# A two-layer hybrid trunk on one core: the second norm stepped into the output product, the second MLP product in another order, the query and key gains in the rotation tables

## The chip, the cores and the metric

The kernel runs as one program on one core of a Trainium2 chip. The metric is the device time of one execution in microseconds. Before the change three runs gave 3245.07, 3245.28 and 3249.05 us, a median of 3245.28 us.

## The reference

The model has two layers over 1024 latent and 256 context tokens of width 1024. Cut to what matters here:

```python
u = modulate(rms_norm(h, norm1_g), shift, scale)
pa, pb, pc, pd = split(u @ w_in)                 # SSD, GQA, RG-LRU, differential attention
q = rms_norm(q.reshape(b, L, H, d), q_g)         # per head; the same for k; for pb and pd
q, k = axial_rope(q, row, col), axial_rope(k, row, col)      # latent tokens only
...
mix = concat([ya, yb, yc, yd]) @ w_out
h = h + mod[2] * mix
v = modulate(rms_norm(h, norm2_g), mod[3], mod[4])
h = h + mod[5] * (square(relu(v @ w_mlp1)) @ w_mlp2)         # D_FF = 4096
```

Context tokens go through the same weights in layer 0 and, for what the latent tokens read of them, in layer 1. All values are float32.

## The kernel before

All work is first recorded as a list of operations and then put in order by a planner, the class `Sched`. The planner gives every operation a cost and a due time: the due time of a TensorE operation is the sum of the TensorE costs recorded before it, and other operations get theirs back from the operations that use their results. It then walks through simulated time, gives each free engine the ready operation that is due first, and emits the instructions in the order so found. So the order of recording isn't the order of execution, but it sets who is due first. All instructions carry line 606, since one helper emits them; they are told apart by tile names.

Tiles come from classes with a fixed number of slots: "S" has 30 wide tiles (1288 columns), "w" six for split weights, "raw" three for weights as loaded, "h" four of 512 columns. A class has quotas by stream of use (line 658 and the following), and a tile may be placed only if enough slots stay free for tiles of other streams that were recorded earlier and aren't placed yet. PSUM banks are given out by stream in the same way.

Every float32 product is made of three products in the fast float32 format: an operand is split into an upper part (`hi`, a copy, on ScalarE or VectorE) and the remainder (`lo`, a subtraction on VectorE), and hi*hi, hi*lo and lo*hi are added up in a PSUM bank. The residual stream h is held as eight tiles hT[k] of 128 features by up to 1280 tokens; tokens come in three groups, 0 and 1 of 512 latent tokens and 2 of 256 context tokens.

The parts that the change touches:

- `attn_proj` (line 1347) computes the projections dtq, kv, dq and dk in tiles of 128 tokens, and `qk_post` (line 1297) does the norm and the rotation of a tile: square on ScalarE, the product of the bank with the gain into b (line 1306), the sum of squares, the power -1/2 on GpSimd, and for latent tokens (t < 8) the products of b with the cosine and the sine table, their sum, the transposes and the split.
- `out_proj` (line 1531) is run twice; the second run ("w2367") holds all eight weight blocks split in the tiles wo and then goes through the groups 0, 1, 2 (0, 1 in layer 1), eight output tiles f in each.
- `norm_halves` (line 1596) follows it. `norm_stats` squares hT and sums over the features with small products, takes the power on GpSimd; `norm_rows` broadcasts the result into a bank. Then the operands of the seven products V0 to V6 of a Strassen-like scheme (2 by 2 by 2 blocks: two feature halves, two token halves) are made: X from group 0, Y from group 1 (tiles vx and vy), V0 and V1 are X, V4 a part of Y, and V2, V3, V5, V6 are differences. In layer 0 the context's operands stand in the last 256 columns of V0, V1, V2 and V4, and their temporaries lx come from class "h".
- `mlp_up` (line 1652) goes through 16 pairs p of column blocks of the first MLP weight. A pair loads two raw tiles, a11 and a12 in one, a21 and a22 in the other, makes the combinations in mt and in place, and does the seven products in the order V0 to V6 of 12 matmuls each, in layer 0 two context products of 24 matmuls of 256 columns as well. Tiles ma, mt, mc and mx of class "h" hold partial sums. Results go to DRAM (hp, hc).
- `mlp_down` (line 1767) does the second product in four quarters q of eight weight blocks, with the seven products named A11, A12, S3, A22, S2, S1, S4 and, for the context, A21. Accumulators are 14 wide tiles ka; operands kb (quota 7) are loaded through hs and split, context operands kc (4) are loaded as they are, weights stand in raw and kr (5). In the last quarter the sums of the accumulators and the additions to h follow, and h is reloaded (`reload_h`, line 1861) from the copy he.
- `mlp` (line 1882) saves h to he, calls `norm_halves`, records the constants of layer 1 in layer 0 (`consts_a`, `consts_b`: rows vrow, of class "h", transposed) and sets the modulation of layer 1 as filling: `raw_tile` takes 0.9 steps of it at every weight load.

Of the kernel before, what the change touches and what calls it, by code (L numbers as in the profile page):

```python
# [647 lines left out]
class Trunk:  # L648
# [4 lines left out]
    def __init__(self, tc, nc, A, out, pools, dbg=None):  # L653
# [4 lines left out]
        s.cls("S", sb, 30, SW, dict(u=16, ssd=8, lru=11, sw=2, qk=4, qv=2, ssdr=1, gk=4, dk=4, gv=2, dv=1, gq=2, dq=1, mo=2, gP=4, dP=8, gT=5, dT=5, mix=16, hT=8, wo=8, v=28, vx=4, vy=4, md=2, ka=14, kb=7, kr=5, kc=4, x=7, wm=10, st=5))  # L658
# [4 lines left out]
        s.psum(ps, dict(mm=(0, 1, 2, 3), m4=(0, 1, 2, 3, 4, 5), ln=(4, 5, 3), att=(3, 0), tr=(6, 7), pv=(6,), ax=(6,),  # L663
# [306 lines left out]
    def norm_stats(self, gi):  # L970
        s = self.s
# [3 lines left out]
        for k in range(0, 8, 2):  # L975
            calls = []
            for j in (k, k + 1):
                sq = s.tile("h", 512, F32, "lq", "sq")
                s.act(sq[:, 0:gn], self.hT[j][:, g0:g0 + gn], AF.Square)
                q = 32 * (j % 4)  # L980
                calls.append(dict(out=st[q:q + 32, 0:gn], lhsT=self.ones32, rhs=sq[:, 0:gn], start=(k < 4),
                                  stop=(k >= 4)))
            s.mms(calls, par=2)
        sts = s.tile("h", 512, F32, "lq", "sts")
# [7 lines left out]
        return m  # L992
# [304 lines left out]
    def qk_post(self, l, bank, off, H, d, gain, t, dst, rq=None):  # L1297
# [8 lines left out]
        s.tt(hd(b), hd(src), gain.un(1).bc([128, H, d]), ALU.mult)  # L1306
# [7 lines left out]
        if t < 8:  # L1314
            j = d // 4
            o = 144 * t + (0 if d == 64 else 96)
            cs = self.rope[:, o:o + d // 2]
            sn = self.rope[:, o + d // 2:o + d + d // 2]
            b4, c4, s4 = (v.r("p (h f k) -> p h f k", h=H, f=2) for v in (b, c, st[:, 0:n]))
            s.tt(c4, b4, cs.un(1).un(1).bc([128, H, 2, 2 * j]), ALU.mult)  # L1320
            s.tt(s4, b4[:, :, ::-1], sn.r("p (f k) -> p f k", f=2).un(1).bc([128, H, 2, 2 * j]), ALU.mult)
            s.tt(b, c, st[:, 0:n], ALU.add)
        y = b
# [23 lines left out]
    def attn_proj(self, l, u, name, tiles):  # L1347
# [6 lines left out]
        v = None  # L1354
        for t in tiles:
            yield (t - tiles[0]) / len(tiles)
            bank = self.gemm_tm(ww, u, t, n, 8 if name == "dtq" and t >= 8 and l == 1 else n)
            if name == "dtq":
                s.copy("ACT", dtraw[:, 8 * t:8 * t + 8], bank[:, 0:8])
                if t < 8 or l == 0:  # L1360
                    self.qk_post(l, bank, 8, 4, 64, L["gqa_q_norm_g"], t, self.qd["gq"], self.rq[:, 12 * t:12 * t + 4])
            elif name == "kv":
                self.qk_post(l, bank, 0, 2, 64, L["gqa_k_norm_g"], t, self.qd["gk"])
                v = self.put_v(v, t, bank[:, 128:256], self.qd["gv"])
            elif name == "dq":
                self.qk_post(l, bank, 0, 8, 32, L["diff_q_norm_g"], t, self.qd["dq"], self.rq[:, 12 * t + 4:12 * t + 12])
            elif name == "dk":
                self.qk_post(l, bank, 0, 8, 32, L["diff_k_norm_g"], t, self.qd["dk"])
# [162 lines left out]
    def out_proj(self, l, gis, ks):  # L1531
# [28 lines left out]
        for f in range(8):  # L1560
# [6 lines left out]
            if late:  # L1567
# [4 lines left out]
                held.append((hi, lo))  # L1572
            else:
# [22 lines left out]
    def norm_halves(self, l, gis):  # L1596
# [21 lines left out]
        bb = self.norm_rows(self.norm_stats(0), 0)  # L1618
        X, Y = [], []
        for k in range(4):  # L1620
            x = s.tile("S", SW, F32, "vx", "vx")
            X.append((x[:, 0:512], x[:, 512:1024]))
# [3 lines left out]
        bb = self.norm_rows(self.norm_stats(1), 1)  # L1626
        bc = self.norm_rows(self.norm_stats(2), 2) if 2 in gis else None
        for k in range(4):
            y = s.tile("S", SW, F32, "vy", "vy")
            Y.append((y[:, 0:512], y[:, 512:1024]))  # L1630
            for j in range(2):
                scaled(Y[k][j], k + 4 * j, 512, 512, 0, bb)
            s.tt(X[k][0], Y[k][0], X[k][0], ALU.subtract)
            put(2, k, X[k][0], None)
            put(4, k, Y[k][1], sh(0, k + 4))
            if bc is not None:
                for j in range(2):
                    z = s.tile("h", 512, F32, "ln", "lx")
                    scaled(z[:, 0:256], k + 4 * j, NL, 256, 1, bc)
                    hi, lo = V[j][k][:, 1024:1280], V[4 - 2 * j][k][:, 1024:1280]  # L1640
                    s.act(hi, z[:, 0:256], AF.Identity, bias=sh(1, k + 4 * j))
                    s.stt(lo, z[:, 0:256], sh(1, k + 4 * j), hi.f, ALU.add, ALU.subtract)
        for k in range(4):
            s.tt(X[k][0], Y[k][1], X[k][0], ALU.subtract)
            put(3, k, X[k][0], sh(0, k + 4))
            s.tt(Y[k][0], Y[k][1], Y[k][0], ALU.subtract)
            put(5, k, Y[k][0], dsh[:, k:k + 1])
            s.tt(X[k][1], X[k][1], X[k][0], ALU.subtract)
            put(6, k, X[k][1], None)
        return V  # L1650

    def mlp_up(self, l, V, gis):


        s, A = self.s, self.A
        w = A["w_mlp1"][l]
        self.hp, self.hc = [], []

        def product(bank, ws, o, first):
            wh, wl = ws  # L1660
            more = {} if first else {"skip_group_check": True}
            for k in range(4):
                c = slice(128 * k, 128 * k + 128)
                xh, xl = V[o][k][:, 0:512], V[o][k][:, 512:1024]
                s.mms([dict(out=bank.v, lhsT=wh[:, c], rhs=xh, start=(first and k == 0), stop=False, **more),
                       dict(out=bank.v, lhsT=wh[:, c], rhs=xl, start=False, stop=False, **more),
                       dict(out=bank.v, lhsT=wl[:, c], rhs=xh, start=False, stop=(first and k == 3), **more)])
# [8 lines left out]
        def context(e, w0, w1, ctx):  # L1676
            pb = bank()
# [15 lines left out]
        for p in range(16):  # L1693
            A2 = []
            for e in range(2):
                raw = self.raw_tile("wr")
                c0 = 128 * (2 * p + e)
                s.dma(raw[:, 0:1024].r("p (k c) -> p k c", k=8), w[:, c0:c0 + 128].rearrange("(k p) c -> p k c", p=128))
# [356 lines left out]
```

## Time and profile before

| | us |
|---|---|
| runs (median of three) | 3245.28 |
| the profiled execution | 3245.98 |
| its span | 3244.2 |
| TensorE busy in the span | 3096.8 |
| VectorE busy | 2434.1 |
| ScalarE busy | 1460.2 |

The span runs from the first to the last instruction of the profiled execution; 1.8 us of its time lie outside. Busy time counts an instruction from its start to its end, with overlaps counted once. [...] Names as in `wa<-wr` are tiles, written and read; a wait is put down to the instruction that released it.

### The profile page before, as it was taken

Reading aid. Unit: us, or ns where it says so; the run is one execution under the profiler, and the core shown is the slowest. Engines: PE = TensorE matmul, PEld = TensorE weight load, DVE = VectorE, ACT = ScalarE, POOL = GpSimd, SP = SyncE. Lnnn points to the kernel's source line nnn. Section 1 sums busy time; section 2 is a strip of 40 time slices with the busy share of each in tenths; the row PEclk is TensorE's granted clock in tenths of the full one; section 3 lists DMA queues with packets and bytes.
Section 4 is the critical chain, followed back from the end, with each engine's and each line's share of the span. In section 5 each row is a group of like instructions: output and inputs, shape, how many; then the busy total and the mean of one; then the engine's idle time right before and its main releaser. Section 6 shows DMA issues by size and latency. Waiting matters only on the chain. (4 is left out here: it accounts for less than half of the span.)

```text
span 3244.2 us, 47231 instructions
## 1 busy us (share of the span) xinstructions
PE 3096.8 (95%) x17688; PEld 2483.1 (77%) x17688; DVE 2434.1 (75%) x4451; ACT 1460.2 (45%) x2658; POOL 148.9 (5%) x168
## 2 busy tenths in 40 slices
PE   8999999899979999999999999999999899999998
PEld 6877886677757777888887688786677577877886
DVE  4797789895476566666779689689895587777888
ACT  5555438774143223343323474347783333345333
POOL 0020040000000000000000010030000000000000
PEclk9999999999979999999999999999999999999999
DMA  8443361416235555552443312242316134465443
GB/s 239 155 135 90 100 182 40 104 43 240 80 106 187 185 183 189 206 167 89 156 154 129 122 61 64 64 117 70 96 58 198 63 130 150 152 208 175 147 142 123
DMA packets 327613, 429.73 MB, mean 132 GB/s; under 512 B 31068, under 2 KB 220376, under 8 KB 327384
## 3 DMA queue, kind: packets, MB, share of 16 engines
q1 hardware_dynamic: 327384, 426.71, 41.1%
q8 instruction: 139, 2.28, 0.3%
q14 instruction: 90, 0.74, 0.1%
HBM read 295.30 MB, written 131.33 MB: 132 GB/s over the span
## 5 line engine op out<-in xcount | busy, mean ns | idle before, releaser
L606 PE MATMUL banks<-v,wa 128*128 128x512 f32 (+1 forms) x3456 | 747.8, 376 | 37.0 <-DVE wa L606 22.1
L606 PEld LDWEIGHTS banks<-v,wa 128*128 128x128 f32 x3456 | 600.9, 191 | 192.6 <-issue 13.6
L606 PE MATMUL banks<-kb,wa 128*128 128x512 f32 x2688 | 651.4, 395 | 1.8 <-ACT ka L606 0.9
L606 PEld LDWEIGHTS banks<-kb,wa 128*128 128x128 f32 x2688 | 493.4, 188 | 113.4 <-ACT ka L606 3.4
L606 ACT ACTIVATE wa<-wr 128x512 fp32r<-128x512 f32 x345 | 210.9, 628 | 395.4 <-PE banks L606 235.4
L606 DVE TENSOR_SCALAR_CACHE_REDUCE P<-banks,rq 128x1280 f32<-128x1280 f32 (+1 forms) x216 | 301.4, 1427 | 32.0 <-PE banks L606 30.3
L606 DVE TENSOR_TENSOR wa<-wr,wa 128x512 fp32r<-128x512 f32 x416 | 274.8, 685 | 38.5 <-ACT wa L606 36.4
L606 ACT ACTIVATE P<-P,am 128x1280 f32<-128x1280 f32 (+1 forms) x216 | 273.4, 1272 | 21.4 <-DVE P L606 19.7
L606 PE MATMUL banks<-wh,uh 128*128 128x256 f32 (+2 forms) x784 | 244.6, 312 | 6.9 <-DVE qkw L606 4.6
L606 PE MATMUL banks<-ks,qt 128*128 128x512 f32 (+1 forms) x800 | 222.2, 389 | 20.6 <-DVE P L606 16.0
L606 PE MATMUL banks<-wl,uh 128*128 128x256 f32 (+2 forms) x784 | 223.2, 285 | 0.0
L606 PE MATMUL banks<-wh,ul 128*128 128x256 f32 (+2 forms) x784 | 222.5, 284 | 0.0
L606 PE MATMUL banks<-uh,wh 128*128 128x512 f32 (+1 forms) x528 | 202.8, 384 | 5.2 <-ACT cvr L606 2.0
L606 PE MATMUL banks<-cst,P 128*128 128x128 f32 x1312 | 189.8, 279 | 17.5 <-ACT PT L606 11.2
L606 PE MATMUL banks<-uh,wl 128*128 128x512 f32 (+1 forms) x528 | 194.1, 368 | 2.4 <-DVE wl L606 2.4
L606 PE MATMUL banks<-ul,wh 128*128 128x512 f32 (+1 forms) x528 | 193.7, 367 | 0.0
L606 PEld LDWEIGHTS banks<-cst,P 128*128 128x128 f32 x1312 | 146.5, 141 | 54.1 <-ACT PT L606 27.1
L606 DVE TENSOR_TENSOR ka<-banks,ka 128x512 f32<-128x512 f32 (+1 forms) x224 | 135.9, 619 | 67.8 <-PE banks L606 66.9
L606 PEld LDWEIGHTS banks<-ks,qt 128*128 128x128 f32 x800 | 134.4, 193 | 62.0 <-DVE P L606 33.1
L606 PEld LDWEIGHTS banks<-wh,uh 128*128 128x128 f32 x784 | 151.1, 193 | 22.7 <-issue 10.1
L606 DVE TENSOR_TENSOR kb<-hs,kb 128x512 fp32r<-128x512 f32 x224 | 152.1, 687 | 19.9 <-ACT kb L606 17.7
L606 ACT ACTIVATE PT<-banks 128x512 f32<-128x512 f32 x259 | 144.9, 596 | 48.5 <-PE banks L606 44.1
(296 smaller groups left out, 4934.3 us busy)
## 6 DMA issues: line engine op xcount, KB each, us to landing
wr<-in_w_mlp_dram SPq DMA_DIRECT2D x128, 512.0 KB
hs<-hp SPq DMA_DIRECT2D x224, 256.0 KB
wm<-in_w_mod_dram SPq DMA_DIRECT2D x96, 512.0 KB
wr<-in_w_in_dram SPq DMA_DIRECT2D x40, 512.0 KB
hp<-me SPq DMA_DIRECT2D x64, 256.0 KB
hp<-mf SPq DMA_DIRECT2D x64, 256.0 KB
ks<-dk SPq DMA_DIRECT2D x64, 160.0 KB
qt<-dq SPq DMA_DIRECT2D x72, 128.0 KB
```

The lines of the kernel that those rows point to most:

```text
L606: getattr(e, method)(**args)
```

## The change

There are three parts.

The norm in steps. `norm_stats` becomes a generator, `stats_steps`, and `norm_halves` one as well. The second output product now does groups 0 and 2 as the weights come, and group 1 last; after each of the eight output tiles of group 1 it saves that tile of h and takes one step of the norm. The rest of the norm (Y, V2 to V6, in this order, for all four k each) is recorded after the first two products ("heads") of pairs 0 and 1. The context's temporaries stand in columns 1024 to 1280 of vx and vy. Constants and modulation of layer 1 begin at pair 2, with 1.1 steps per weight load. Context products get their own order of banks ("cx").

The second product of the MLP has the order A11, A21, S3, S2, S1, A22, A12, S4; S2 is made in place of A21 and S4 beside S1. Five of the seven sums per m of the last quarter follow S1; A22 is followed by two additions to h, A12 and S4 by one each.

`rope_gain` multiplies the rotation tables with the gain once per projection and layer into a wide tile rg (quota 2); `qk_post` then multiplies the bank itself with these tables, and makes the product with the gain only for context tokens.

```diff
+    def rope_gain(self, gain, d):
+        w = s.tile("S", SW, F32, "rg", "rg")
...
+        for f in range(2):
+            s.tt(cg[:, :, f], tab[:, :, o:o + h], g[:, f].un(1).bc([128, 8, h]), ALU.mult)
+            s.tt(sg[:, :, f], tab[:, :, o + h * (1 + f):o + h * (2 + f)], g[:, 1 - f].un(1).bc([128, 8, h]), ALU.mult)
...
-        s.tt(hd(b), hd(src), gain.un(1).bc([128, H, d]), ALU.mult)
+        if t >= 8:
+            s.tt(hd(b), hd(src), gain.un(1).bc([128, H, d]), ALU.mult)
...
-            b4, c4, s4 = (v.r("p (h f k) -> p h f k", h=H, f=2) for v in (b, c, st[:, 0:n]))
-            s.tt(c4, b4, cs.un(1).un(1).bc([128, H, 2, 2 * j]), ALU.mult)
+            b4, c4, s4 = (v.r("p (h f k) -> p h f k", h=H, f=2) for v in (src, c, st[:, 0:n]))
+            s.tt(c4, b4, rg[0][:, t].un(1).bc([128, H, 2, 2 * j]), ALU.mult)
...
+                for gi in gis:
+                    if gi != 1:
+                        add(f, held[f], gi)
...
         if late:
-            for gi in gis:
-                for f in range(8):
-                    add(f, held[f], gi)
+            self.norm2 = self.norm_halves(l, gis)
+            self.hd2 = [s.dram(128, NT, f"he{l}_{k}") for k in range(8)]
+            for f in range(8):
+                add(f, held[f], 1)
+                s.dma(self.hd2[f][:, 0:n], self.hT[f][:, 0:n])
+                next(self.norm2)
...
+    def mlp_heads(self, l):
+        return [self.up_head(l, p, p == 0) for p in range(2)]
...
+            a11, a12, tail, a, w11, w12, px = heads.pop(0) if heads else self.up_head(l, p)
+            if l == 0 and p == 2:
+                self.consts_a(1, self.norm_end)
+                self.consts_b(1, self.norm_end)
+                self.fill, self.fill_rate = itertools.chain(*[self.mod_round(1, r) for r in range(3)]), 1.1
...
-            for i, name in enumerate(("A11", "A12", "A21", "S3", "A22", "S2", "S1", "S4")):
+            for i, name in enumerate(("A11", "A21", "S3", "S2", "S1", "A22", "A12", "S4")):
...
-                    if h is None and name == "A22":
+                    if h is None and name == "S1":
                         self.reload_h(n)
...
-        V = self.norm_halves(l, gis)
+        next(self.norm2)
+        heads = self.mlp_heads(l)
+        next(self.norm2)
```

## Rows read from the trace of the kernel before

**Rows 1.** Page, part 1: busy us (share of the span) xinstructions of each engine.
```profile
PE 3096.8 (95%) x17688; PEld 2483.1 (77%) x17688; DVE 2434.1 (75%) x4451; ACT 1460.2 (45%) x2658; POOL 148.9 (5%) x168
```

**Rows 2.** Stretches: busy us (xinstructions) by engine, granted TensorE clock, DMA share, GB/s.
```profile
895.00:905.00 10.00, 7.12 (x39) 3.71 (x39) 4.76 (x9) 3.42 (x10) 1.01 (x1) 0.83 0.49 172
905.00:925.00 20.00, 11.40 (x36) 8.50 (x37) 19.36 (x40) 10.28 (x19) 1.07 (x1) 0.57 0.01 3
925.00:945.00 20.00, 8.18 (x25) 6.32 (x24) 19.05 (x32) 10.93 (x20) 0.00 (x0) 0.66 0.08 20
2565.00:2575.00 10.00, 8.33 (x42) 4.91 (x41) 9.42 (x16) 6.88 (x12) 1.35 (x1) 1.00 0.26 107
2575.00:2590.00 15.00, 9.47 (x23) 5.18 (x22) 14.87 (x24) 5.17 (x8) 0.00 (x0) 0.66 0.00 1
2590.00:2610.00 20.00, 11.81 (x40) 7.89 (x38) 19.96 (x33) 10.95 (x19) 0.00 (x0) 0.83 0.19 53
1785.00:1800.00 15.00, 11.02 (x35) 4.15 (x31) 12.92 (x21) 7.11 (x13) 2.22 (x2) 0.66 0.21 58
3150.00:3224.00 74.00, 74.00 (x332) 60.10 (x331) 70.63 (x117) 23.54 (x40) 0.00 (x0) 1.00 0.33 104
3224.00:3244.00 20.00, 8.71 (x44) 6.03 (x42) 10.38 (x17) 6.74 (x12) 0.00 (x0) 0.69 0.42 157
```

**Rows 3.** TensorE groups from 3000 and from 1400 us: xcount, busy, mean ns.
```profile
L606 PE MATMUL banks<-kb,wa 128*128 128x512 f32 x218 | 50.7, 394 | 0.0
...
L606 PE MATMUL banks<-kc,wa 128*128 128x256 f32 x569 | 85.2, 281 | 0.0
```

**Rows 4.** Timeline, second norm of layer 0: start, us, engine, operation, [idle <-releaser].
```profile
901.76 3.38 DVE L606 SCALAR_TENSOR_TENSOR vy<-hR,gs,banks 128x512 f32<-128x512 f32 x5 [3.01 <-PE banks L606]
...
921.28 0.34 SPq L606 DMA_DIRECT2D vrow<-in_b_mod_dram  x1
...
937.41 0.69 DVE L606 TENSOR_TENSOR mt<-wr 128x512 f32<-128x512 f32 x1
...
938.71 8.59 PE L606 MATMUL banks<-v,wa 128*128 128x512 f32 x24 [11.82 <-DVE wa L606]
```

**Rows 5.** VectorE groups, 901.7 to 937 us.
```profile
L606 DVE SCALAR_TENSOR_TENSOR vy<-hR,gs,banks 128x512 f32<-128x512 f32 x8 | 5.6, 742 | 3.0 <-PE banks L606 3.0
...
L606 DVE SCALAR_TENSOR_TENSOR v<-lx,mod,v 128x256 fp32r<-128x256 f32 x8 | 3.6, 476 | 0.0
...
L606 DVE SCALAR_TENSOR_TENSOR lx<-hR,gs,banks 128x256 f32<-128x256 f32 x8 | 3.6, 474 | 0.6 <-PE banks L606 0.6
```

**Rows 6.** Timeline of layer 1's second norm.
```profile
2565.29 0.97 PE L606 MATMUL banks<-mx,wo 128*128 128x512 f32 x3
...
2575.06 3.38 DVE L606 SCALAR_TENSOR_TENSOR vy<-hR,gs,banks 128x512 f32<-128x512 f32 x5 [0.19 <-PE banks L606]
```

**Rows 7.** VectorE groups of the query and key norms, whole kernel.
```profile
L606 DVE TENSOR_TENSOR qkw<-qkw,rope 128x256 f32<-128x256 f32 x96 | 36.8, 421 | 1.3
...
L606 DVE TENSOR_TENSOR qkw<-banks,bc 128x256 f32<-128x256 f32 x56 | 23.3, 418 | 10.6 <-ACT qkw L606 10.0 <-DMA dq<-qkw 0.6
...
L606 DVE TENSOR_TENSOR qkw<-qkw,rope 128x128 f32<-128x128 f32 x32 | 8.3, 289 | 0.0
```

**Rows 8.** Waits of TensorE, whole kernel: us in total, times, longest us.
```profile
PE banks L606 <- DVE qkw L606: 10.6, 9, 2.5
```

**Rows 9.** Timeline of the kernel's end.
```profile
3220.49 3.05 PE L606 MATMUL banks<-kb,wa 128*128 128x512 f32 x12
...
3224.18 4.89 DVE L606 TENSOR_TENSOR ka<-ka,ka 128x512 f32<-128x512 f32 x8
...
3228.99 5.38 DVE L606 SCALAR_TENSOR_TENSOR hR<-ka,mod,hR 128x512 f32<-128x512 f32 x8
```

**Rows 10.** Timeline of SyncE's queue at the end of layer 0: reloads of h.
```profile
1728.11 0.32 SPq L606 DMA_DIRECT2D hR<-he  x1
...
1728.95 16.13 SPq L606 DMA_DIRECT2D hR<-he  x7
```

More of the change, by code (lines that the diff above doesn't have):

```diff
@@ L1625, in norm_halves @@
                 put(j, k, X[k][j], sh(0, k + 4 * j))
-        bb = self.norm_rows(self.norm_stats(1), 1)
-        bc = self.norm_rows(self.norm_stats(2), 2) if 2 in gis else None
+        steps = self.stats_steps(0)
+        for k in range(4):
+            next(steps)
+        yield
+        m = next(steps)
+        yield
+        bb = self.norm_rows(m, 0)
+        first(0)
+        yield
+        first(1)
+        steps = self.stats_steps(2) if 2 in gis else iter([None] * 5)
+        next(steps), next(steps)
+        yield
+        first(2)
+        next(steps), next(steps)
+        yield
+        first(3)
+        mc = next(steps)
+        yield
+        steps = self.stats_steps(1)
+        next(steps), next(steps)
+        yield
+        next(steps)
+        yield
+        next(steps)
+        m = next(steps)
+        bc = self.norm_rows(mc, 2) if 2 in gis else None
+        bb = self.norm_rows(m, 1)
+        self.V = V
+        yield
         for k in range(4):
@@ L1634, in norm_halves @@
             put(2, k, X[k][0], None)
+            if bc is not None:
+                for j in range(2):
+                    scaled(Z[j][k], k + 4 * j, NL, 256, 1, bc)
+        for k in range(4):
+            s.tt(X[k][0], Y[k][1], X[k][0], ALU.subtract)
+            put(3, k, X[k][0], sh(0, k + 4))
+        for k in range(4):
             put(4, k, Y[k][1], sh(0, k + 4))
@@ new lines, in up_product @@
+    def up_product(self, bank, o, ws, first):
+        s, V = self.s, self.V
+        wh, wl = ws
+        more = {} if first else {"skip_group_check": True}
+        for k in range(4):
+            c = slice(128 * k, 128 * k + 128)
+            xh, xl = V[o][k][:, 0:512], V[o][k][:, 512:1024]
+            s.mms([dict(out=bank.v, lhsT=wh[:, c], rhs=xh, start=(first and k == 0), stop=False, **more),
+                   dict(out=bank.v, lhsT=wh[:, c], rhs=xl, start=False, stop=False, **more),
+                   dict(out=bank.v, lhsT=wl[:, c], rhs=xh, start=False, stop=(first and k == 3), **more)])
@@ new lines, in up_raw, with up_head @@
+    def up_raw(self, l, c):
+        raw = self.raw_tile("wr")
+        self.s.dma(raw[:, 0:1024].r("p (k c) -> p k c", k=8),
+                   self.A["w_mlp1"][l][:, 128 * c:128 * c + 128].rearrange("(k p) c -> p k c", p=128))
+        return raw[:, 0:512], raw[:, 512:1024]
+    def up_head(self, l, p, both=True):
+        s = self.s
+        a11, a12 = self.up_raw(l, 2 * p)
+        tail = self.up_raw(l, 2 * p + 1) if both else None
+        a = s.tile("h", 512, F32, "ma", "ma").v
+        w11 = self.halves(a11)
+        px = s.tile("psum", 512, F32, "m4", "pg")
+        self.up_product(px, 0, w11, True)
+        s.copy("ANY", a, px.v)
+        w12 = self.halves(a12)
+        self.up_product(px, 1, w12, False)
+        return a11, a12, tail, a, w11, w12, px
@@ L1657, in mlp_up @@
+    def mlp_heads(self, l):
+        return [self.up_head(l, p, p == 0) for p in range(2)]
+    def mlp_up(self, l, heads, gis):
+        s, V = self.s, self.V
         self.hp, self.hc = [], []
         def product(bank, ws, o, first):
[L1660 to L1667, printed above, removed]
+            self.up_product(bank, o, ws, first)
@@ L1676, in context @@
         def context(e, w0, w1, ctx):
-            pb = bank()
+            pb = s.tile("psum", 512, F32, "cx", "pg")
             o = pb[:, 0:256]
```

123 lines of the change are left out of this document (57 added, 66 removed).

## The prediction

> **What bounds the kernel now.** I began with the page's busy shares: TensorE is busy 95% of the span, VectorE 75% [rows 1]. A kernel whose TensorE is that full gains only where TensorE is idle or at its lower clock, so next I read busy time by stretch [rows 2]: in nearly every stretch of the two MLP products TensorE is busy for all of it, with VectorE behind it, and three places stand out.
>
> First, the second norm of layer 0 (895 to 945 us). [...] In the same stretch VectorE is full (19.36 and 19.05 of 20).
>
> Second, the same place in layer 1 (2565 to 2610): 29.6 of 45 busy, 15.4 idle, at the lower clock 3.2 + 2.0 lost: 20.6 us.
>
> Third, the seams: layer 0 to layer 1 (1785 to 1800: 4.0 idle and some 3.7 at the lower clock) and the end of the kernel (3224 to 3244). Elsewhere the full rate is 50.7 us for 218 matmuls of 512 columns, 233 ns each, and 85.2/569 = 150 ns for 256 columns [rows 3]. So one product of the seven in a pair (12 matmuls) is 2.8 us and one context product (24 of 256) 3.6 us.
>
> The timeline says what holds layer 0 up [rows 4]: VectorE works on the operands of the norm from 901.76 without a break, the sum of two weight blocks (mt) that the third product needs only comes at 937.41, and TensorE has by then waited 11.82 us for it. mt, ma, mx, the norm's lx and the vrow rows of the next layer's constants (DMA from 921.28) all come from one class "h" of four tiles (line 661). With ma, mx and two vrow tiles alive, mt has none. That is my reading of the code; the wait is measured.
>
> **The change, part by part.**
>
> *Norm inside the output product.* The VectorE work of the norm isn't reduced: per layer 8 vy at 742 ns, the X differences, 20 lower halves, and in layer 0 the 16 context steps (3.6 + 3.6 us) [rows 5]. What changes is the cover and the order. (a) All of group 0's operands and statistics come under group 1's output product, which is now last; (b) the first two products of pairs 0 and 1 (4 products, 11.2 us) are recorded ahead of the rest of the norm; (c) the rest comes in the order in which the pair eats it, V2, V3, V4, V5, V6; (d) the context's temporaries leave class "h" and the constants of layer 1 wait until pair 2, so mt finds a tile.
>
> From the last output matmul to the first vy there is a chain (square, two small products, power, broadcast) which in layer 1 takes 2575.06 - 2566.26 = 8.8 us [rows 6]; I assume the same after the change in both layers. Then VectorE needs 937.41 - 901.76 = 35.6 us in layer 0, and 35.6 - 7.2 = 28.4 in layer 1, without the context steps. About five steps of pair 0 at 0.69 us (row mt) fall among them: 3 us. TensorE is full again about one loop (8 steps, 5 us) before the last operand, because pair 1 has work by then.
> Layer 0: 8.8 + 35.6 + 3 - 5 = 42.4 us, in which TensorE has four head products (11.2), V2 to V5 (11.2), two context products (7.2) and about 2 of statistics, 31.6 in all. Loss 10.8, with 5 for the lower clock (8.9 before, with far fewer matmuls between the gaps) and 2 because four weight tiles of six stay held until the context products: 18 instead of 32.2, **a gain of 14** (bounds: 6, half of the 11.82 wait alone; 21, no lower clock and no shortage).
> Layer 1: 8.8 + 28.4 + 3 - 5 = 35.2 us against 11.2 + 11.2 + 2 = 24.4, loss 10.8, with 4 for the lower clock 15 instead of 20.6, **a gain of 5** (0 to 10). Here pair 1's first products already served as filling, late; so less is to be had.
>
> The eight saves of h (he, 640 KB each) move into the output product's loop. They are on SP's queue ahead of the first weights of the MLP; the weights of the heads are needed only some 10 us later. Nothing. The modulation of layer 1 starts at pair 2 at 1.1 steps per weight load instead of 0.9: the same steps later and denser, through the three raw tiles that the pairs use as well. Nothing, with 3 us to either side.
>
> *Query and key norms.* For 64 of the 76 tiles the product with the gain goes: 48 of 256 columns at 418 ns and 16 of 128 at 289 (row of the same shape) are 24.7 us of VectorE. Added are four products for each of 4 projections and 2 layers: 16 of 256 elements (421) and 16 of 128 (289), 11.4 us [rows 7]. Net 13.3 us less, and the chain ahead of the transposes is one step shorter. TensorE waits 10.6 us for qkw in the whole kernel [rows 8], so 10 is the upper bound, 0 the lower; half of it, **5**, since VectorE is the fuller engine there but most of the waits end with it being late on other work too.
> The two rotation products now read the PSUM bank instead of SBUF. The rows show no difference: 418 ns from the bank, 421 from SBUF, both 256 columns [rows 7]. [...]
>
> *Second MLP product reordered.* Matmuls, splits and sums are the same in number (28 sums, 16 additions to h in the last quarter, in both orders). After the last product the kernel now does 4 + 8 + 8 VectorE steps until about 3234.4 (2.8 us of them ahead of the rows shown), then half of the final transposes [rows 9]. After the change only 4 + 4 depend on the last product, and the upper half of h is finished two products earlier: at most 4.89 + half of 5.38 = 7.6 us less. But VectorE is full in the whole last quarter (70.63 of 74 us from 3150 to 3224 [rows 2]) and its work isn't less, so what moves forward pushes something else back: 0 is the other bound. I take **4**.
> In layer 0 the order has a price. The 30 wide tiles are all named: 14 ka, 7 kb, 5 kr, 4 kc (line 658). The context operands kc were free after the fifth product, where h is reloaded into 8 of these tiles; now they are held to the seventh. The reload, which took 16.13 us for its last seven tiles [rows 10], is then fed by kb and two ka tiles, and the allocator lets no later kb in before all eight are placed: one kb is left for the sixth product, so its four operands are split one after another. That is four times about 1.4 us (two steps of 0.69), less what the context products cover: **a loss of 4** (0; 17 if three products suffer, 12 operands). The seam into layer 1 gets group 0 one product later but is bound by VectorE, whose work is the same: nothing, 5 to either side.
>
> **Sum**, against the profiled execution's own 3245.98 us (0.7 above the median of 3245.28): - 14 - 5 - 5 - 4 + 4 = - 24, so **3222 us**. All bounds together give 3197 and 3257.
>
> **The rivals.**
> *The gaps are VectorE's, not the order's.* If the planner's order fills TensorE no better, because VectorE's 35.6 and 28.4 us stand and the heads only move from the end of the gap to its start, layer 0 gains just half of the mt wait (6) and layer 1 nothing: - 6 - 0 - 5 - 0 + 4 = 3239 us. For it: pair 1's heads already filled the end of layer 1's gap. Against: 11.82 us of waiting in layer 0 for one 0.69 us step. Chance 0.2.
> *Slower: the new table tile takes a tile from the projections.* rg is up to two more wide tiles while u (16), rope (1), ssd (8), qk and qv share the 30, so the ring qk falls from three or four tiles to two. A tile lives through some eight VectorE steps of 0.42 (3.4 us) and about as much again on ScalarE, GpSimd, the transposes and a DMA, with queueing by estimate 9 us; two tiles then give one token tile per 4.5 us, while its matmuls take 24 x 0.150 = 3.6. At 0.9 us on the 38 tiles of dtq and kv, next to SSD, it costs 34, the query gain is gone, and the time is 3222 + 5 + 34 = 3261. It decides from about 0.65 us per tile on (25 us, which makes 3252). Against it: SSD doesn't hold its eight all the time. Chance 0.08.
> *The reload starves layer 0's end.* 17 instead of 4, with the VectorE-bound tail giving 0: 3222 + 13 + 4 = 3239, and the seam 5 more, 3244: no change. Chance 0.1.
>
> **How the numbers follow.** Forecast 0.6, the rule on PSUM reads (3226) 0.02; rivals 0.2, 0.08, 0.1. The range 3200 to 3250 leaves out only the slot rival and the corners of the bounds. A measurement of this kernel can tell about 0.2%, 6.5 us: faster is below 3238.8. Of the first rival half lies below that, of the reload a third: faster 0.62 + 0.1 + 0.03 = 0.75, same 0.1 + 0.07 = 0.17, slower 0.08.
>
> **What would show it.** In the profile after: the loss around layer 0's norm near 18 us and no wait of 10 us on wa; layer 1's near 15; TensorE's waits on qkw about half of 10.6; the last hR additions about 2 us behind the last product; around the reload in layer 0 short waits on kb. Wrong it would be if the norm's gaps stay above 28 and 20, if the projections get longer, or if TensorE waits for kb by tens of us.

## The result, and the profile after

The change made the kernel slower. The changed kernel takes 3265.56 us (median of five runs, 3264.38 to 3267.25), the kernel before, run beside it, 3249.05 us: a ratio of 1.0054, with a 95% interval of 1.0037 to 1.0070. Forecast were 3222 us and a range of 3200 to 3250. The profiled execution took 3264.38 us with a span of 3262.6 us, 18.4 us more than the span before.

To see where they lie I cut both spans at the same instructions (first or last start of a group of matmuls, from the view by tile): the first transposes of the attention, the last product of the MLP's first weight (v, wa), the last of its second (kb, wa), the first projection of layer 1 (uh).

| stretch, us | before | after | difference |
|---|---|---|---|
| layer 0: start, projections | 484.0 | 501.4 | +17.4 |
| attention, output product, norm, first MLP product | 892.7 | 888.0 | -4.7 |
| second MLP product | 407.6 | 419.3 | +11.7 |
| seam to layer 1 | 14.1 | 4.9 | -9.2 |
| layer 1: projections | 405.6 | 421.8 | +16.2 |
| attention to first MLP product | 704.0 | 694.8 | -9.2 |
| second MLP product | 315.1 | 320.5 | +5.4 |
| end | 21.1 | 11.9 | -9.2 |

So five terms of the forecast are there to be seen, and one, the projections, has the wrong sign and 33.6 us.

Page, part 1, of the changed kernel; beside [rows 1] VectorE has 21.0 us less to do, and TensorE, with the same 17688 matmuls, is busy 17.1 us longer:

```profile
PE 3113.9 (95%) x17688; PEld 2493.8 (76%) x17688; DVE 2413.1 (74%) x4396; ACT 1474.0 (45%) x2681; POOL 147.2 (5%) x168
```

The mean granted clock, 0.980 before and 0.981 after, doesn't explain that by itself (last section). Three stretches in the projections before (span, TensorE's busy us, granted clock, DMA share, GB/s):

```profile
150.00:200.00 50.00, 45.67 (x302) 1.00 0.56 173
1900.00:1950.00 50.00, 44.85 (x252) 0.86 0.26 80
1950.00:2000.00 50.00, 48.87 (x292) 1.00 0.22 67
```

and after, followed by the two of layer 0's norm, its reload and layer 1's norm, which answer to [rows 2]:

```profile
150.00:200.00 50.00, 39.96 (x231) 0.90 0.50 159
1900.00:1950.00 50.00, 38.86 (x229) 0.90 0.21 69
1950.00:2000.00 50.00, 43.16 (x249) 0.86 0.28 85
916.00:936.00 20.00, 17.10 (x74) 0.90 0.05 18
936.00:956.00 20.00, 15.61 (x59) 0.76 0.11 29
1740.00:1760.00 20.00, 10.74 (x41) 0.78 0.79 267
2611.00:2631.00 20.00, 14.71 (x46) 0.85 0.09 27
```

In these 150 us of the projections TensorE is idle 17.4 us more than before (139.4 busy against 122.0), and where the clock was full (1.00) it is now 0.90 and 0.86, and in the stretch between them it rose from 0.86 to 0.90. At the norms it is much better filled: 4.4 of 20 us idle at the worst in layer 0, where 11.8 were. At 1740 us there is a hole that the kernel before does not have.

TensorE's waits over the whole kernel (us in total, times, longest), to be held against [rows 8]:

```profile
PE banks L606 <- DVE qkw L606: 20.3, 10, 5.6
...
PE banks L606 <- DVE wa L606: 10.4, 10, 2.2
PE banks L606 <- ACT kb L606: 8.9, 1, 8.9
```

The wait on qkw has doubled instead of halving. No wait on wa is longer than 2.2 us, where one of 11.82 stood [rows 4]. One wait of 8.9 us on kb is new. How a wait on qkw comes about, in the timeline of the changed kernel, on ScalarE, VectorE and TensorE:

```profile
1934.63 0.28 PE L606 MATMUL banks<-wh,ul 128*128 128x264 f32 x1
...
1958.90 0.36 ACT L606 ACTIVATE qkw<-banks 128x256 f32<-128x256 f32 x1
...
1958.18 2.32 DVE L606 TENSOR_TENSOR_SCAN q<-a,q,th 128x1024 f32<-128x1024 f32 x1
1960.42 0.73 DVE L606 TENSOR_TENSOR qkw<-banks,rg 128x256 f32<-128x256 f32 x2
...
1961.29 0.36 PE L606 MATMUL banks<-wh,uh 128*128 128x264 f32 x1 [3.62 <-DVE qkw L606]
```

The last of the 24 matmuls into this bank ends at 1934.9. ScalarE squares the bank only at 1958.90 and is done at 1959.26. VectorE is in a scan of another branch until 1960.5, then does the two rotation products, which now read the bank, one behind the other. The next projection starts right behind them, after 3.62 us idle: the bank was what it lacked. Of the 26 us for which the bank stood full, 24 lie ahead of the square, the first step that reads it; the second rotation product adds less than half a microsecond.

The hole at 1740 us, on SyncE's queue of the changed kernel, beside [rows 10]:

```profile
1736.51 13.64 SPq L606 DMA_DIRECT2D hR<-he  x7
1753.44 0.38 SPq L606 DMA_DIRECT2D wr<-in_w_in_dram  x1
1753.87 7.36 SPq L606 DMA_DIRECT2D hs<-hp  x3
```

The next operands of the product (hs) are asked for only after the last reload; TensorE stands 8.91 us for the first kb made from them.

The end, beside [rows 9]:

```profile
3252.30 1.40 DVE L606 SCALAR_TENSOR_TENSOR hR<-ka,mod,hR 128x512 f32<-128x512 f32 x2
```

The last additions to h are these two, done at 3253.7, where eight ran from 3228.99 to 3234.37, and the first stores of the output leave at 3245.15.

### The profile page after: what moved, and what is told of

Same layout as the page of the kernel before. It is cut to its first block, busy times and chain, and to the rows that moved or that the text cites. A ratio compares the mean times of both kernels' runs of the same rounds, so it can differ in the third digit from the quotient of the medians.

```text
span 3262.6 us, 47245 instructions
## 1 busy us (share of the span) xinstructions
PE 3113.9 (95%) x17688; PEld 2493.8 (76%) x17688; DVE 2413.1 (74%) x4396; ACT 1474.0 (45%) x2681; POOL 147.2 (5%) x168
## 5 line engine op out<-in xcount | busy, mean ns | idle before, releaser
L606 ACT ACTIVATE P<-P,am 128x1280 f32<-128x1280 f32 (+1 forms) x216 | 273.4, 1272 | 22.1 <-DVE P L606 20.3
L606 PE MATMUL banks<-wh,uh 128*128 128x256 f32 (+2 forms) x784 | 248.2, 317 | 19.9 <-DVE qkw L606 17.4
L606 PE MATMUL banks<-cst,P 128*128 128x128 f32 x1312 | 189.5, 279 | 17.3 <-ACT PT L606 10.6
```

Source lines behind the costliest of these rows:

```text
L606: getattr(e, method)(**args)
```

## The experiments

My theory after these lines was that the third part costs some 33 us, by the wide tile rg that it takes from the projections (the slot rival of the prediction). The rival to it: the price is not the tile, but that the bank is held until both rotation products are done. All ratios are to the kernel before, run beside each.

### The third part, taken to pieces

**e1: the third part alone**, the class's `rg=2`, `rope_gain` and the edits of `qk_post` and its callers.

> The kernel before with the third part alone: rope_gain, the wide tile rg, and the rotation products taken from the bank. My theory now (the slot): rg holds one of the 30 wide tiles in all four projections, and ring qk and the tiles of the neighbouring stages get one less; in the two traces the first attention transposes come 17 us later in layer 0 and another 16 us later in layer 1. It expects 3249 + 33 = 3282 us (3270 to 3292), all of it between the first projection and the attention. Rival (the loss lies in how the norm's and the projections' parts meet): 3249 - 5 = 3244 us.

Measured: 3274.88 us, ratio 1.0084 (1.0069 to 1.0099): +27.7 us. The projections are longer by 13.1 and 16.3 us, everything else is within 2 us. The third part explains the loss by itself.

**e2: the tile alone.** The steps of before, and rg held from the first to the last rotated tile of each projection by two GpSimd steps of four columns:

```diff
+            if t in (0, 7):
+                s.pool("tensor_tensor", rate=165, out=rg[:, 0:4], in0=b[:, 0:4], in1=self.nhalf[:, 0:4], op=ALU.mult)
...
+            rg = s.tile("S", SW, F32, "rg", "rg")
```

> The kernel before, unchanged in what it computes, but a wide tile rg is held from the first to the eighth token tile of each query and key projection (two GpSimd operations of about 1 us each per projection write four columns of it, 16 in the whole kernel). No VectorE operation is added or taken away. Slot theory: most of the 33 us return without any of the other edits, 3270 to 3284 us. Rival (the bank is held longer, because both rotation products now read PSUM and the next user of the bank waits): no change, 3244 to 3254 us.

Measured: 3280.82 us, 1.0101 (1.0082 to 1.0119): +33.7 us. In the profiled execution, the slowest of four with 3286.64 us, 24.3 and 13.7 us lie in the two projections. One wide tile held through the projections is enough for a loss of this size, with no step of VectorE changed. TensorE's wait on qkw is then as long as in the changed kernel (20.3), though as before only the gain's product reads the bank on VectorE:

```profile
PE banks L606 <- DVE qkw L606: 21.2, 15, 5.2
```

**e3: no tile, no gain.** The rotation products read the bank and the tables as they are; the gain is left out of the result.

```diff
-        s.tt(hd(b), hd(src), gain.un(1).bc([128, H, d]), ALU.mult)
+        if t >= 8:
+            s.tt(hd(b), hd(src), gain.un(1).bc([128, H, d]), ALU.mult)
...
-            b4, c4, s4 = (v.r("p (h f k) -> p h f k", h=H, f=2) for v in (b, c, st[:, 0:n]))
+            b4, c4, s4 = (v.r("p (h f k) -> p h f k", h=H, f=2) for v in (src, c, st[:, 0:n]))
```

> The kernel before with the rotation products taken from the bank and the product with the gain left out for latent tokens (the gain of the query and key norms is left out there, nothing stands in its place): 24.7 us of VectorE work less, no table, no tile rg. Slot theory: as before or a little faster, 3240 to 3250 us. Rival (bank held longer): 3265 to 3282 us.

Measured: 3256.71 us, 1.0028 (1.0017 to 1.0039): +9.6 us. It lies between the ranges of the two theories, and is against the tile as the only cause: with 24.7 us less on VectorE and no tile the kernel is still slower, and TensorE waits more for qkw than the 10.6 us of [rows 8]:

```profile
PE banks L606 <- DVE qkw L606: 13.0, 8, 3.3
```

**e8: the same, copied first.** As e3 (the gain of the latent tiles is left out), but ScalarE copies the bank into b and the products read b. Against e3, beside b in place of src in the products:

```diff
+        else:
+            s.act(b, src, AF.Copy)
```

> The kernel before with the gain left out, as in the run without gain, but ScalarE first copies the bank, and the two rotation products read the copy. The gain is left out of the result (of the first eight token tiles). No table, no tile, 24.7 us less on VectorE and about the same more on ScalarE. Theory: the run without gain was 9.6 us slower because the bank stays held until the second rotation product, after the sum of squares and two small steps on VectorE; with the copy the bank is free after two ScalarE steps, so this is as fast as before or faster: 3232 to 3247 us, 3240. Rival: any change of VectorE's steps here disturbs the order of the projections by about 10 us, or the reads of a bank were not it: 3253 to 3260.

Measured: 3230.21 us, 0.9938 (0.9914 to 0.9961): 19.4 us faster than before, below the expected range, and 29.0 less than e3 by the differences to before. The wait on qkw in this kernel:

```profile
PE banks L606 <- DVE qkw L606: 4.2, 6, 1.3
```

Between e3 and e8 VectorE's work is the same (2411.8 and 2411.5 us busy, rotation products of 256 columns of 417 and 418 ns on the mean); what differs is that the bank is free after two steps of ScalarE. So it is worth 29 us here to let ScalarE free the bank, and the steps taken from VectorE are worth more than I gave them once the bank no longer waits for it. That is not yet the price of the second rotation product, since before the change the bank waited for VectorE as well.

**e9: the third part alone, copied first**: tables, tile and gain as in e1, the copy as in e8.

> The kernel before with the third part alone, as in the first run, but ScalarE first copies the bank into the work tile and the two rotation products read the copy: the table's wide tile is there, the bank's long hold is not. Two prices have been measured apart so far: a wide tile held through each projection +33.7 us (the run with the tile alone), the bank held until both products 9.6 + 19.4 = 29 us (without gain, without and with the copy). Theory: both prices are there in the third part and overlap, so the copy takes back part: against before 3247 to 3249, 3258 (3250 to 3266), that is 10 to 24 us less than the third part as it is (+27.7). Rival 1: the tile is all, the copy changes nothing, 3272 to 3280. Rival 2: the bank is all, 3232 to 3247.

Measured: 3246.57 us, 1.0003 (0.9990 to 1.0015). The copy takes back the whole loss of e1. My theory (3258) missed; the time lies in the range of the second rival, the bank. With e9 these four kernels make a square, in differences to before:

| us | bank held (products read it) | copied first |
|---|---|---|
| no tables, gain left out | +9.6 (e3) | -19.4 (e8) |
| tables in a wide tile | +27.7 (e1) | +0.5 (e9) |

The copy is worth 29.0 and 27.2 us, the tables with their tile cost 18.1 and 19.9, of which their 32 products, 11.4 us of VectorE by [rows 7], can be a part. In these totals the two prices add up, by layer they don't: the tables with their tile cost 3.0 and 12.0 us in the projections of layers 0 and 1 without the copy and 0.3 and 20.1 with it, and the tile alone cost 24.3 in layer 0 (e2). In e9 TensorE's waits have moved to ScalarE's use of the work tile, in total and in number:

```profile
PE banks L606 <- ACT qkw L606: 13.7, 8, 3.8
PE banks L606 <- DVE qkw L606: 5.9, 7, 1.8
```

**e12: a ring of three.** One tile less for these steps, none held: `qk=4` becomes `qk=3`.

> The kernel before with the work tiles of the query and key steps in a ring of three instead of four, nothing else: a wide tile of the shared class is free, and one less may be in use by this part. It tells whether the price of the table's tile is that of one tile fewer in the class, or that of one fewer for these steps. Theory: the class of 30 is full in the projections, and a tile fewer for the query and key steps costs less than a tile held through all of it, since the others may use it: 3255 us (3247 to 3265). Rival: the query and key steps are what sets the pace there, so that it costs as much as the held tile: 3270 to 3285.

Measured: 3253.27 us, 1.0020 (1.0010 to 1.0029): +7.2 us. One tile fewer in the ring, which the other streams may use, costs a fifth of one that is held. But this is a sum of opposites: the projections of layer 0 are 17.1 us longer, near the 17.4 of the changed kernel, and those of layer 1 are 4.7 us shorter. A tile fewer can hardly make a stage faster by itself, so the planner's order alone seems to move a stage by some 5 us; that much is not to be read as a price. Why the held tile costs 33.7 in e2 and some 18 to 20 with the tables stays open; the kernels differ in VectorE's work too, and no run held the tile in e8.

**How long the banks stand full.** The traces say which end of the hold each edit changes. For the 76 token tiles of these projections, matched in their order, I took the time from the last matmul into the bank to the square, and from the square to the end of the last read by these steps (in the example above the next projection starts 0.14 us behind an end so found). Sums in us:

| kernel | last matmul to square | square to last read |
|---|---|---|
| before | 333 | 224 |
| e3: two reads, no tile | 326 | 247 |
| e2: tile held, one read | 440 | 203 |
| e1: third part, tile and two reads | 429 | 208 |
| changed kernel | 432 | 208 |
| e8: copied first, no tile | 363 | 79 |
| e9: third part, copied first | 428 | 77 |

The tile delays the square, the step that first writes the work tile, by about 100 us in all, of which 92 in the changed kernel fall on the 38 tiles of dtq and kv, the two that the slot rival named. The second read adds 23 us behind the square where there is no tile, and nothing in the changed kernel. The copy takes some 130 us off the other end, and that end was as long before the change. So the copy pays for the tile's delay in another place; that it is worth 27 to 29 us does not say that the second read costs as much.

**e13: the changed kernel, whole, copied first.**

> The changed kernel, whole, with one edit: ScalarE first copies the bank into the work tile, and the two rotation products with the tables read the copy. Theory: as in the third part alone, where the same edit took back 27 us, the long hold of the bank is what made the change slower; the tables' wide tile stays as a price of about 19 us, paid by the 24.7 us of gain products that are gone. Expected 3237 us, the time of the changed kernel without the third part (3228 to 3246). Rival: in the whole kernel the tile decides, since the two projections now begin later and the order is another: 3250 to 3266.

Measured: 3237.90 us, 0.9976 (0.9964 to 0.9987). The one added ScalarE step per tile turns the change from 0.54% slower to 0.24% faster, to what the changed kernel takes without its third part (e4), as expected.

### The other two parts

**e4: the changed kernel without its third part.**

> The changed kernel with the third part undone (the query and key norms as before), the norm in steps and the reordered second product kept. If the parts add up, 3265.6 - 33 = 3232 us (3224 to 3240), that is 17 us less than before: some 3 from layer 0's norm, 9 from layer 1's, 4 to 9 from the end. If the parts hurt each other, 3245 to 3260.

Measured: 3237.41 us, 0.9965 (0.9950 to 0.9980). The projections are back (+3.0 and -1.4 us), the rest as in the table of the changed kernel.

**e5: the norm in steps alone.**

> The kernel before with the first part alone: the norm in steps inside the output product, the first halves' product ahead, the context products on their own banks, the modulation filler started later at 1.1. In the changed kernel without the third part, the span from the output product to the last norm-fed instruction came 6 us sooner in layer 0 and 8 us sooner in layer 1, and the rest of its 9.7 us was the second part's. Theory: the two norms are independent of the second product, so this alone gives -14 us, 3233 us beside 3247 (3225 to 3241). Rival: the second part's early end in layer 1 is where the gain really is, and the norm's gain is given back in the up product, whose TensorE lost 3 to 4 us more than before; then 3242 to 3250.

Measured: 3231.64 us, 0.9946 (0.9926 to 0.9966): -17.9 us, in the profiled span -12.7: 4.5 in layer 0 from the attention to the first MLP product, 1.1 each at the second product and the seam, 6.2 in layer 1.

**e6: the second product's order alone.**

> The kernel before with the second part alone: the order of the second MLP product's blocks. In the changed kernel the TensorE stood 8.91 us in layer 0's last quarter for an operand behind the reload of the hidden rows, the product ended 12 us later, 9 us of it came back at the seam to layer 1, and the end of the kernel came 9 us sooner after the last product but that product ended 5 us later. Theory: these add to about zero, 3247 us (3240 to 3254), with the stall of about 9 us in layer 0 there again. Rival: the tail's gain is whole and the seam gives all back, then 3236 to 3240.

Measured: 3247.58 us, 0.9995 (0.9985 to 1.0006): no change. The stretches are +12.2 (layer 0's second product), -9.2 (seam), +4.6 (layer 1's) and -9.2 (end), the pattern of the changed kernel, with the same hole:

```profile
1744.92 0.79 PE L606 MATMUL banks<-kb,wa 128*128 128x512 f32 x1 [8.93 <-ACT kb L606]
```

**e7: norm in steps, order in layer 1 alone**, no third part; layer 0 keeps the old order of the second product.

> The changed kernel without the third part, and with the second part in layer 1 alone: layer 0's second product keeps the order of before. Theory: layer 0's order costs 12.7 us at its end and gives 9 us at the seam, so leaving it at the old order gives 3 to 4 us against the changed kernel without the third part (3237): 3234 us, range 3226 to 3240, and no stall of TensorE over 2 us for an operand at layer 0's end. Rival: the seam's gain is worth more than the stall, because the stall lies where the next work waits anyway; then 3240 to 3248.

Measured: 3230.43 us, 0.9945 (0.9923 to 0.9966). The hole is gone; the seam is 14.3 us again and layer 0's second product 407.6. Its interval and e4's overlap, so what the order in layer 0 costs beside the norm is not settled, and beside e5 the order in layer 1 gains nothing that shows.

**e14 and e15: the filler.** e14 is e5 with the modulation filler at 0.9 steps per weight load (the second edit alone), e15 has filler and constants at the first pair as well, as before:

```diff
-            if l == 0 and p == 2:
+            if l == 0 and p == 0:
...
-                self.fill, self.fill_rate = itertools.chain(*[self.mod_round(1, r) for r in range(3)]), 1.1
+                self.fill, self.fill_rate = itertools.chain(*[self.mod_round(1, r) for r in range(3)]), 0.9
```

> The norm in steps alone (3231.6 us), with the modulation filler of layer 1 starting at the third pair as there, but at 0.9 steps per weight load as before instead of 1.1. Theory: the 4 to 5 us that TensorE loses more in the up product behind the norm come from the denser filler, which shares VectorE and ScalarE's evictions and the raw tiles with the pairs: at 0.9 up to 4 us are won there, and what is left of the filler runs after the pairs: 3230 us (3224 to 3238). Rival: the filler then isn't through when the up product ends, and its rest stands in the open: 3238 to 3248.

> The norm in steps alone (3231.6 us), with layer 1's constants and the modulation filler in their old place (the first pair) and at the old rate of 0.9. Theory: the constants' four vrow tiles and filler evictions then fall again among the norm's last operands, where they took the class of four small tiles from the weight sums: TensorE's wait for wa of some 10 us at the norm comes back, and 5 to 11 us are lost: 3240 us (3236 to 3246). Rival: the reordered operands alone made the gain, the filler's place is nothing: 3228 to 3235.

Measured: e14 3241.30 us, 0.9986 (0.9974 to 0.9998); e15 3240.78 us, 0.9983 (0.9970 to 0.9995). Both lose some 0.4%, most of e5's gain; in e14 the rival was right, not my theory. In e14 TensorE's loss between 1000 and 1300 us is smaller (4.4 us idle against 7.4 in e5), but the filler runs to 1362 us instead of 1300, and at the start of the second MLP product its operands come late; the wait in that stretch (820 to 1400 us):

```profile
PE banks L606 <- ACT kb L606: 8.5, 1, 8.5
```

So the rate of 1.1 has a price in the up product and is worth it. In e15 the norm's hole is back. Two stretches of e5, then of e15:

```profile
905.00:925.00 20.00, 14.58 (x48) 0.78 0.00 0
925.00:945.00 20.00, 15.98 (x67) 0.84 0.14 34
```

```profile
905.00:925.00 20.00, 9.68 (x39) 0.74 0.00 0
925.00:945.00 20.00, 3.03 (x14) 0.59 0.08 20
```

and the timeline of e15 at its end:

```profile
944.03 0.69 DVE L606 TENSOR_TENSOR mt<-wr 128x512 f32<-128x512 f32 x1
...
945.33 1.19 PE L606 MATMUL banks<-v,wa 128*128 128x512 f32 x2 [9.72 <-DVE wa L606]
```

This is the picture of [rows 4], mt late and a long wait for wa, with all of the reordering of the operands in place. In e14, with constants and filler at the third pair and the old rate, the norm is as in e5 (165.69 and 164.70 us busy from 820 to 1000). So layer 0's gain at the norm hangs on where the constants and the filler of layer 1 stand; the order of the operands alone does not bring it, and which of the two it is, constants or filler, no run separates. Layer 1's 7.0 us are there in e15 too.

### Two versions that beat both kernels

**e10: e7 with the bank copied first**, the gain still on VectorE, out of the copy; nothing is left out:

```diff
-        s.tt(hd(b), hd(src), gain.un(1).bc([128, H, d]), ALU.mult)
+        s.act(b, src, AF.Copy)
+        s.tt(hd(b), hd(b), gain.un(1).bc([128, H, d]), ALU.mult)
```

**e11: the same with that product on GpSimd.**

> The kernel of the run with the second part in layer 1 alone and the norm in steps (3230.4 us), with the gain kept on VectorE but out of a copy that ScalarE makes of the bank first: the bank is held by two ScalarE steps instead of one of each engine; VectorE has as many steps as before, ScalarE 76 more of about 0.38 us. Theory: of the 19.4 us that the copied-first run without gain gained, the earlier release of the bank is a part and the 24.7 us less on VectorE the other; here only the first is there: 3222 us (3212 to 3231). Rival: the release of the bank was no limit in the order of before (its gain product comes right behind the square), all of the 19.4 us was VectorE's work: 3230 to 3238.

> As the run before it, with the gain's product (76 of at most 128x256) on GpSimd out of ScalarE's copy: VectorE is rid of all 24.7 us of gain products on the tiles, with no table and no wide tile. Theory: GpSimd is idle 95% of the time and the step is not the last of its chain, since the power of the sum of squares comes later: 3212 us (3202 to 3228). Rival: GpSimd's product is slow (no such row in the trace of before; its 128x1024 memset took 0.95 us, a power of 8 elements 1.7 us) and the powers queue behind it, so that the bank of the transposition and the work tile are held longer: 3232 to 3250.

Measured: e10 3224.15 us, 0.9928 (0.9904 to 0.9952); e11 3227.74 us, 0.9935 (0.9919 to 0.9950). e10 is the fastest that computes everything: 22 us under the kernel before. Against e7 it is a step in the expected direction, but the intervals overlap; so do those of e10 and e11, and e11 is at the upper end of what was expected. On GpSimd the product of 256 columns takes twice VectorE's 418 ns [rows 7]:

```profile
L606 POOL TENSOR_TENSOR qkw<-qkw,bc 128x256 f32<-128x256 f32 x56 | 48.0, 860 | 278.3 <-ACT qkw L606 207.6 <-DVE wk L606 53.5 <-DVE gw L606 7.5
```

VectorE is rid of 76 products, 28.9 us, but is busy only 1.7 us less (2422.3 against 2424.0), since other steps of it have become longer, by 21.7 us in the sum of their durations (the group that grew most is in the last section). So nothing that shows is won by it.

## Why the prediction was wrong

**Query and key norms: the step that failed.** I put the third part at -5 (0 to -10); in the changed kernel the projections take 33.6 us more, alone it costs 27.7 (e1). This term was made of VectorE's work (13.3 us less) and bounded by TensorE's waits on qkw in the kernel before (10.6 us), from which a loss was shut out: a bound from waits holds only while the change makes no new ones, and these went to 20.3. Two things stood in it at nothing.

The first is the wide tile rg. It was in the slot rival, which was to decide from 0.65 us per tile on and had 0.08; against it stood only that SSD does not hold its eight all the time, a sentence without a row. Its 3261 is the nearest to the measured 3265.56. e2 shows the tile alone at +33.7 beside the rival's 34, and the delay of the squares lies on dtq and kv, where the rival had put it. Its ring of fewer tiles is borne out in layer 0 (+17.1 in e12) and not in layer 1 (-4.7).

The second is how long a bank is held. I priced the move of the rotation products to the PSUM bank by their duration alone, and that was right: 417 ns from the bank after the change, 421 from SBUF before [rows 7]. I did not ask when the bank comes free. The reads from the bank lose time even without the tile and with 24.7 us less on VectorE (+9.6, e3), and to free the bank by a copy takes the whole loss back (e9, e13). How the 27.7 us divide between the tile and the second read stays open: the tile costs 33.7 alone and 18 to 20 beside the tables, and in the changed kernel the bank is held longer ahead of the square, not behind it.

No run shows the term that the forecast of 3226 (0.02) rested on: a rotation product of 256 columns takes 417 ns from the bank in e3 and 418 from the copy in e8. The copy was worth 27 us here all the same, by the bank's earlier release; that forecast was about durations and missed it.

**Norm of layer 0: right mechanism, wrong size.** -14 (6 to 21); -4.7 measured in the changed kernel, -4.5 alone, outside the bounds. The long wait on wa went, as forecast, when the constants left class "h" at the norm; e15, with constants and filler back, brings it back. At the norm itself the gain is there: between 820 and 1000 us TensorE is busy 155.72 us before and 164.70 in e5. But from 1000 to 1400 it falls from 396.40 to 392.49: the filler, later and denser, which I had put at nothing, takes 3.9 back there, 3.0 of them by its rate (e14), and 8.5 us at the start of the second product if it is left at 0.9. The 32.2 us that the forecast's sum has as lost at the norm before (18 after) are, by [rows 2], 23.3 of 50 us idle and 8.9 for the clock, an estimate (busy time times what the granted clock lacks of 1) that no run shows by itself; by the same estimate the changed kernel loses 15.9 us from 916 to 966 us, 9.0 idle and 6.9 for the clock (its last 10 us are 8.31 busy at 0.83). In the whole stretch of the table TensorE is idle 8.3 us less in the changed kernel, but busy 3.6 us longer with the same 4931 matmuls, although at a higher clock (0.99 against 0.98); that I had not counted on.

**Norm of layer 1:** -5 (0 to 10); -9.2 measured, 6.2 to 7.8 in e5 and e7. Within the bounds, near the upper one.

**The end: right in sum, in part by luck.** -3.8 together, forecast -4 with the reason that VectorE is full and what moves forward pushes something else back: 9.2 us less behind the last product, 5.4 more in the product before it. But I had bounded the first by 7.6, and taken 4 as about the middle of 0 and 7.6.

**Layer 0's reload:** +4 (0 to 17); the product is 11.7 us longer, 8.91 of them one wait for kb, three operand loads behind the reload, which is the third rival's mechanism. The seam, which I had at nothing with 5 to either side, gives 9.2 back. Together +2.5, near the +4, but by two wrong terms that happen to cancel. With the old order in layer 0 both are gone (e7: 407.6 and 14.3 us); why the seam gets shorter no run shows.

By the forecast's own terms with the measured sizes: -4.7 - 9.2 + 33.6 - 3.8 + 2.5 = +18.4 us. The first rival (gaps that stay with VectorE) is out in layer 1, where it gave nothing; in layer 0 its 6 is nearer to 4.7 than my 14, but the gap itself closed, to 4.4 of 20 us idle at the worst.

## What to carry to other kernels

When a change touches the steps that read a PSUM bank, price the bank's hold from the last matmul to the last read, not only the readers' durations; the wait until the first reader has a tile to write to belongs to it, and was the larger part here (432 us of 640 in the changed kernel). A copy by an engine with room can be worth more than the step that the change saves (27.2 us from e1 to e9, against 13.3 us less of VectorE's work by [rows 7]). What a remedy is worth is not what the fault costs: look in the trace at which end of the wait each of them moves. A tile held through a stretch in which the pool is full has a price even if no step of the work changes (33.7 us in e2), and a run that holds one for nothing measures it. A bound taken from waits of the kernel before says nothing on waits that the change itself makes (10.6 us before, 20.3 after).

## What the runs showed that I had not expected

TensorE's busy time is no constant of the work: the same 17688 matmuls are busy 3096.8 us before, 3113.9 in the changed kernel and 3116.4 in e2. Most of the 18.4 us of the changed kernel stand in the page as busy time. In e2 that is mainly the clock: its mean is 0.975 against 0.980, and TensorE is busy for 128.1 us at the lower level of its granted clock, 0.50, against 97.0. At 0.50 thirteen matmuls of 512 columns, one behind the other, took 5.57 us in the kernel before (938.71 to 944.28 us), 428 ns each, against 233 at 1.00 [rows 2 and 3]. By that 46% of the difference, 14.2 us, is lost, of 19.6. In the changed kernel TensorE is busy for 111.5 us at the lower level, which gives 6.6 of the 17.1 us. The rest, most of it from the attention to the first MLP product, stays open.

Some of VectorE's steps are longer with the products on GpSimd: with the gain's product there (e11) VectorE's step on eight sums takes more than twice as long as with that product on VectorE (e10). The group in e10:

```profile
L606 DVE TENSOR_SCALAR qkm<-qkm 128x8 f32<-128x8 f32 x38 | 6.3, 165 | 0.3
```

and in e11:

```profile
L606 DVE TENSOR_SCALAR qkm<-qkm 128x8 f32<-128x8 f32 x38 | 14.4, 378 | 0.9
```

GpSimd's powers are in both kernels; what e11 adds there is the gain's 76 products. By which way they lengthen VectorE's step from 165 to 378 ns no run here shows.
